# Two SBUF tiles for the exponentials of a two-map attention, and the keys' other 64 rows written by an SBUF-to-SBUF transfer

## The chip, the core and the metric

The kernel runs on one core of a Trainium2 chip. The metric is the device time of one execution in microseconds (us). TensorE (PE) does the matrix products, VectorE (DVE), ScalarE (ACT) and GpSimd (POOL) the elementwise work, and SyncE (SP) issues the transfers. Each engine runs its own instruction list in order and waits on semaphores. [...]

## The reference, cut to what matters

Two transformer blocks follow each other: `first_block` with two layers on 512 latent and 256 context tokens, and `second_block` with one layer. The change touches only the attention of `first_block`: 8 heads in each of the two layers, each head with two softmax maps of 64 dimensions whose difference weighs the values.

```python
def _diff_attn(qb, k_all, v_all, lam):
    s = jnp.einsum('bqhid,bkhid->bhiqk', qb.astype(jnp.float32) * ATTN_SCALE, k_all.astype(jnp.float32))
    p = jax.nn.softmax(s, axis=-1)
    a = p[:, :, 0] - lam * p[:, :, 1]
    return jnp.einsum('bhqk,bkhe->bqhe', a.astype(v_all.dtype), v_all)

def _diff_subln(o, g, lam_init):
    of = o.astype(jnp.float32)
    y = of * lax.rsqrt(jnp.mean(jnp.square(of), axis=-1, keepdims=True) + RMS_EPS) * g * (1.0 - lam_init)
    return y.reshape(o.shape[0], o.shape[1], D_ATTN).astype(o.dtype)
...
    y_attn = jax.nn.silu(ag) * _diff_subln(att, subln_g_l, lam_init)
```

Keys are the 256 context and the 512 latent ones, 768 together. In layer 0 the context tokens have queries too, which see the 256 context keys alone; layer 1 has latent queries only.

## The kernel before

A number is kept as the sum of a high and a low fp32r part, and a product is three matmuls. `unit` (L198) is one such projection: 48 matmuls of 128x512 for the latent tokens into a PSUM tile of tag `ps_m` and, where context is wanted, 48 of 128x256 into another. `ps_m` has four buffers; the score tile `ps_s`, the transposition tile `ps_t` and the output tile `ps_v` have one each.

`attention` (L465) goes over the heads. For each it makes four units (queries, keys, values, gate), evicts them (`evict_q`, `evict_k`, `evict_v`, and L487 for the gate `SG`), and calls `attend`. The order of instructions on every engine is set at compile time by a scheduler with its own timing estimates. It lays the four units of head h+1 among the score rounds of head h: PE works on them while DVE and ACT do a softmax. These matmuls (L166) are called the fill here. The weights of the fill are split into parts by ACT (`whi`, L159) and POOL (`wlo`, L139); a reduction for later gates (`gpr`, L802 on POOL and L803 on ACT) runs along.

A score round is one map of one tile of 128 queries: two or four score matmuls into `ps_s` (L394), the maximum on DVE (L399), its multiple (L401), the exponential on ACT (L408), the reciprocal of the sum (L410). Map 0's exponentials go to an SBUF tile `E0` with two buffers; map 1's are written in place into `ps_s`. L415 and L416 make the weighted difference, L416 reading `ps_s`, so that the score tile is free only after L416. The difference is transposed on PE (L423), split (L427, L428) and multiplied with V (L433). A head of layer 0 has eight rounds of 768 keys, called long, and then four of 256 keys, called context rounds; a head of layer 1 has eight long ones.

`evict_k` writes four tiles for a head, each with one buffer: KH0 and KH1 hold the high part of a map's 64 dimensions in both halves of the partitions, KL0 and KL1 the low part. ACT writes two halves (L350, L351), DVE casts the other two (L352, L353) and makes all four low halves (L139 under L355, L356). Since the tiles have one buffer, they are written after the last scores of the head before. The source `qr` and the tile `vT` of `evict_v` share one buffer too, so that L360, which reads the value unit out of `ps_m`, waits for the last of these DVE operations, and the fill that needs this `ps_m` buffer (the gate unit's, then the next head's) waits for L360.

At the end of a head, the sum of squares of 256 queries comes from two matmuls with ones (L446, L447); then follow L453 and a square root on ACT (L455), reciprocals on DVE (L460), a product into `SG` (L461) and a store (L463). `SG` has one buffer: the next head's gate (L251) waits for that store, and the `ps_m` buffer that L251 reads is awaited by a value unit of the fill. [rows 8] shows that chain.

Of the kernel before, what the change touches and what calls it, by code (L numbers as in the profile page):

```python
# [11 lines left out]
F32 = mybir.dt.float32  # L12
F32R = mybir.dt.float32r
BF16 = mybir.dt.bfloat16
AF = mybir.ActivationFunctionType
ALU = mybir.AluOpType
# [7 lines left out]
NT = NL + NCX  # L24
# [21 lines left out]
def mixer_stack_kernel(ctx: ExitStack, tc: tile.TileContext, a: dict, out: bass.AP):  # L46
    nc = tc.nc
# [14 lines left out]
    def ps_s():  # L62
        return pp.tile([128, 2, 512], F32, name="ps_s", tag="s", bufs=1)

    def ps_t():
        return pp.tile([128, 512], F32, name="ps_t", tag="t", bufs=1)

    def ps_v():
        return pp.tile([128, 512], F32, name="ps_v", tag="v", bufs=1)
# [68 lines left out]
    def sub_lo(lo, src, hi, eng):  # L138
        eng.tensor_tensor(lo, src, hi.bitcast(F32), op=ALU.subtract)  # L139
# [182 lines left out]
    def rope(tp, dst, ps):  # L322
        sh = tp.tile([128, NL], F32, name="rsh", tag="rsh", bufs=1)
        nc.vector.stream_shuffle(sh, ps, SWAP16)
        nc.vector.tensor_tensor(dst, ps, rope_c, op=ALU.mult)
        nc.gpsimd.tensor_tensor(sh, sh, rope_s, op=ALU.mult)
        nc.gpsimd.tensor_tensor(dst, dst, sh, op=ALU.add)
# [14 lines left out]
    def evict_k(ap_, aq, u):  # L342
        kr = aq.tile([128, NT], F32, name="qr", tag="qr", bufs=1)
        rope(aq, kr[:, NCX:], u.lat)
        nc.scalar.copy(kr[:, :NCX], u.cx)
        KH0 = ap_.tile([128, NT], F32R, name="KH0", tag="KH0", bufs=1)
        KH1 = ap_.tile([128, NT], F32R, name="KH1", tag="KH1", bufs=1)
        KL0 = ap_.tile([128, NT], F32R, name="KL0", tag="KL0", bufs=1)
        KL1 = ap_.tile([128, NT], F32R, name="KL1", tag="KL1", bufs=1)
        nc.scalar.copy(KH0[0:64], kr[0:64])  # L350
        nc.scalar.copy(KH1[64:128], kr[64:128])  # L351
        nc.vector.tensor_copy(KH0[64:128], kr[0:64])  # L352
        nc.vector.tensor_copy(KH1[0:64], kr[64:128])  # L353
        for half in (slice(0, 64), slice(64, 128)):
            sub_lo(KL0[half], kr[0:64], KH0[0:64], nc.vector)  # L355
            sub_lo(KL1[half], kr[64:128], KH1[64:128], nc.vector)  # L356
        return (KH0, KL0), (KH1, KL1)

    def evict_v(ap_, u, vT):
        nc.scalar.copy(vT[:, NCX:], u.lat)  # L360
# [15 lines left out]
    def attend(ap_, l, h, Q, K, V, SG, T):  # L376
        Q0, Q1 = Q
        Vh, Vl = V
        for qp in range(T // 256):
            nkt = 6 if qp < 2 else 2  # L380
            nk = nkt * 128
            ncol = nk // 2 if nkt == 6 else nk
            nch = nk // ncol
            aTh = ap_.tile([128, 6, 256], F32R, name="aTh", tag="aTh", bufs=1)
            aTl = ap_.tile([128, 6, 256], F32R, name="aTl", tag="aTl", bufs=1)
            for qi in range(2):
                q0 = qp * 256 + qi * 128
                es, ds = [], []
                for m, (Qm, Km) in enumerate(((Q0, K[0]), (Q1, K[1]))):
                    ps = ps_s()  # L390
                    for c in range(nch):
                        o = ps[:, c, :ncol]
                        for i, kp in enumerate(Km):
                            nc.tensor.matmul(  # L394
                                o, Qm[:, q0:q0 + 128], kp[:, c * ncol:(c + 1) * ncol], start=i == 0, stop=i == 1
                            )
                    sv = ps[:, :nch, :ncol]
                    mx = ap_.tile([128, 1], F32, name="mx", tag="mx", bufs=4)
                    nc.vector.reduce_max(mx, sv, axis=AX.XY)  # L399
                    nb = ap_.tile([128, 1], F32, name="nb", tag="nb", bufs=4)  # L400
                    nc.vector.tensor_scalar(nb, mx, -0.125, None, op0=ALU.mult)  # L401
                    if m == 0:
                        e = ap_.tile([128, NT], F32, name="E0", tag="E0", bufs=2)
                        e = e[:, :nk].rearrange("p (c n) -> p c n", c=nch)
                    else:
                        e = sv
                    d = ap_.tile([128, 1], F32, name="dn", tag="dn", bufs=4)
                    nc.scalar.activation(e, sv, AF.Exp, bias=nb, scale=0.125, accum_out=d)  # L408
                    r = ap_.tile([128, 1], F32, name="rd", tag="rd", bufs=4)
                    nc.vector.reciprocal(r, d)  # L410
                    es.append(e)
                    ds.append(r)
                nc.vector.tensor_tensor(ds[1], ds[1], neglam[l], op=ALU.mult)
                E0, E1 = es
                nc.vector.tensor_scalar(E0, E0, ds[0], None, op0=ALU.mult)  # L415
                nc.vector.scalar_tensor_tensor(E0, E1, ds[1], E0, op0=ALU.mult, op1=ALU.add)  # L416
                kt_of = lambda kt: E0[:, kt * 128 // ncol, kt * 128 % ncol:kt * 128 % ncol + 128]
                for r in range((nkt + 2) // 3):
                    n = min(3, nkt - 3 * r)
                    tp = ps_t()  # L420
                    for i in range(n):
                        kt = 3 * r + i
                        nc.tensor.transpose(tp[:, i * 128:(i + 1) * 128], kt_of(kt), ident)  # L423
                    tv = tp[:, :n * 128].rearrange("p (k d) -> p k d", k=n)
                    dh = aTh[:, 3 * r:3 * r + n, qi * 128:(qi + 1) * 128]
                    dl = aTl[:, 3 * r:3 * r + n, qi * 128:(qi + 1) * 128]
                    nc.scalar.copy(dh, tv)  # L427
                    nc.vector.tensor_tensor(dl, tv, dh.bitcast(F32), op=ALU.subtract)  # L428
            ov = ps_v()
            o = ov[:, :256]  # L430
            for kt in range(nkt):
                for p, (v, t) in enumerate(((Vh, aTh), (Vh, aTl), (Vl, aTh))):
                    nc.tensor.matmul(  # L433
                        o, v[:, kt], t[:, kt], start=(kt == 0 and p == 0), stop=(kt == nkt - 1 and p == 2)
                    )
            y = SG[:, qp * 256:(qp + 1) * 256]
            nc.vector.scalar_tensor_tensor(y, o, subg[l], y, op0=ALU.mult, op1=ALU.mult)
            o2 = ap_.tile([128, 256], F32, name="o2", tag="o2", bufs=1)
            nc.scalar.square(o2, o)
            o2h = ap_.tile([128, 256], F32R, name="o2h", tag="o2h", bufs=1)  # L440
            o2l = ap_.tile([128, 256], F32R, name="o2l", tag="o2l", bufs=1)
            nc.scalar.copy(o2h, o2)
            sub_lo(o2l, o2, o2h, nc.vector)
            msv = ps_v()
            ms = msv[:, :256]
            nc.tensor.matmul(ms, ones_r, o2h, start=True, stop=False)  # L446
            nc.tensor.matmul(ms, ones_r, o2l, start=False, stop=True)  # L447
            if qp == 0:
                rt = ap_.tile([128, 512], F32, name="rt", tag="rt", bufs=1)
                nc.scalar.copy(rt[:, :256], ms)  # L450
                continue
            r = slice(256, 512) if qp == 1 else slice(0, 256)
            nc.scalar.copy(rt[:, r], ms)  # L453
            n = 512 if qp == 1 else 256
            nc.scalar.activation(rt[:, :n], rt[:, :n], AF.Sqrt, bias=eps_t, scale=8.0)  # L455
            for i in range(n // 256):
                q0 = (0, 256)[i] if qp == 1 else 512
                ri = rt[:, i * 256:(i + 1) * 256]
                y = SG[:, q0:q0 + 256]
                nc.vector.reciprocal(ri, ri)  # L460
                nc.vector.tensor_tensor(y, y, ri, op=ALU.mult)  # L461
            o = 0 if qp == 1 else 512
            nc.sync.dma_start(Yd[4 + h][:, o:o + n], SG[:, o:o + n])  # L463
# [245 lines left out]
    with pool("start", R) as sp:  # L709
# [53 lines left out]
        for k in range(KT):  # L763
            hf = sp.tile([128, NT], F32, name="hf0", tag="hf0", bufs=2)
            for i, (nm, o, n, dst) in enumerate(halves):
                nc.vector.scalar_tensor_tensor(
                    hf[:, o:o + n], dst[k][:, 0].bitcast(F32), mods[nm][:, k:k + 1], dst[k][:, 1].bitcast(F32),
                    op0=ALU.add, op1=ALU.add,
# [524 lines left out]
```

## Time and profile before

| | |
|---|---|
| median of 3 runs | 3666.74 us (3661.18 to 3671.53) |
| profiled execution | 3662.99 us, span 3661.2 us |
| mean granted PE clock | 0.95 of 2.4 GHz |
| busy share | PE 90%, DVE 69%, POOL 56%, ACT 42% |
| attention, layer 0 | about 300 to 1150 us of the span |
| attention, layer 1 | about 1700 to 2350 us of the span |

A row of a timeline gives start, length, engine, line, operation, tile written <- tiles read, shapes, and in brackets the idle time before it with the instruction that ended it. Rows of waits give the waiting engine and tile, the releaser, then total us, times and longest.

### The profile page before, as it was taken

How to read it: one execution, taken by the hardware profiler on the slowest of the kernel's cores; microseconds unless marked ns; L12 is line 12 of the kernel's file. 1: busy time of each engine (PE TensorE's matmuls, PEld its weight loads, DVE VectorE, ACT ScalarE, POOL GpSimd, SP SyncE). 2: the span in 40 equal slices, each digit the busy share in tenths (PEclk: the TensorE clock that was granted, in tenths of full speed). 3: DMA queues.
4: the chain of work that ended last, by engine and by line, in shares of the span. 5: the costliest groups of instructions: out<-in, count | busy, mean ns of one | idle time of the engine just before them, and what ended most of it. 6: DMA issues, size and time to landing. Idle time of an engine off the chain costs nothing.

```text
span 3661.2 us, 47866 instructions
## 1 busy us (share of the span) xinstructions
PE 3285.1 (90%) x16462; PEld 2749.9 (75%) x16462; DVE 2541.2 (69%) x3849; ACT 1543.7 (42%) x3208; POOL 2054.8 (56%) x1420
## 2 busy tenths in 40 slices
PE   5879888889988879999999999999989899999987
PEld 4668677778877767777888888877768787878765
DVE  9994565565547888865555665477566889986676
ACT  4433655666433113233556554422445333335343
POOL 6665666777323453245777773478766544444432
PEclk8889899999999989999999999999999999999999
DMA  7542332233115556664444432287766222222575
GB/s 258 207 164 79 105 98 91 92 98 96 53 64 166 172 167 223 190 221 150 138 146 137 142 124 73 84 304 279 230 221 206 97 89 87 90 81 91 180 226 194
DMA packets 269140, 541.03 MB, mean 148 GB/s; under 512 B 30080, under 2 KB 37088, under 8 KB 260704
## 3 DMA queue, kind: packets, MB, share of 16 engines
q1 hardware_dynamic: 268896, 537.97, 45.0%
q8 instruction: 129, 2.11, 0.2%
q14 instruction: 115, 0.94, 0.1%
HBM read 508.05 MB, written 29.80 MB: 147 GB/s over the span
## 4 chain that ended last, share of the span: by engine, by line
PE 40%; DVE 26%; DMA 12%; issue 9%; POOL 9%; ACT 5%; SPq 1%; POOLq 0%; DVEq 0%; ACTq 0%
PE ps_m L166 30%; DVE acc L985 5%; DMA wraw<-in_w_out_dram 5%; POOL wlo L139 4%; DVE gpr L806 4%; POOL gpr L802 3%; DVE gjunk L292 2%; PE ps_s L394 2%; DVE wlo L139 2%; DMA gw<-in_w_ada_dram 2%; PE ps_v L433 1%; DVE h L139 1%; ACT whi L159 1%; PE ps_m L624 1%; PE ps_m L625 1%
## 5 line engine op out<-in xcount | busy, mean ns | idle before, releaser
L139 POOL TENSOR_TENSOR wlo<-wraw,whi 128x512 fp32r<-128x512 f32 x760 | 1120.2, 1491 | 936.5 <-ACT whi L159 819.8
L166 PE MATMUL ps_m<-h,whi 128*128 128x512 f32 (+1 forms) x4608 | 1571.3, 400 | 67.9 <-ACT vT L360 50.4
L166 PEld LDWEIGHTS ps_m<-h,whi 128*128 128x128 f32 x4608 | 880.4, 193 | 258.4 <-ACT vT L360 52.0
L159 ACT CAST whi<-wraw 128x512 fp32r<-128x512 f32 x1032 | 602.7, 618 | 790.9 <-DMA wraw<-in_w_out_dram 264.8
L166 PE MATMUL ps_m<-h,wlo 128*128 128x512 f32 (+1 forms) x2304 | 919.4, 400 | 0.1
L802 POOL TENSOR_TENSOR gpr<-gw,gv 128x512 f32<-128x512 f32 x320 | 429.6, 1342 | 242.5 <-ACT gpr L803 187.6
L166 PEld LDWEIGHTS ps_m<-h,wlo 128*128 128x128 f32 x2304 | 444.3, 193 | 93.6 <-POOL wlo L139 0.5
L166 PE MATMUL ps_m<-hc,whi 128*128 128x256 f32 x1920 | 510.4, 283 | 0.0
L139 DVE TENSOR_TENSOR wlo<-wraw,whi 128x512 fp32r<-128x512 f32 x272 | 240.4, 896 | 182.0 <-ACT whi L159 179.3
L166 PEld LDWEIGHTS ps_m<-hc,whi 128*128 128x128 f32 x1920 | 356.9, 191 | 4.0
L803 ACT ACTIVATE gpr<-gpr 128x512 f32<-128x512 f32 x320 | 201.6, 630 | 243.9 <-POOL gpr L802 243.1
L166 PE MATMUL ps_m<-hc,wlo 128*128 128x256 f32 x960 | 271.6, 283 | 0.0
L806 DVE SCALAR_TENSOR_TENSOR gpr<-gw,gv 128x512 f32<-128x512 f32 x264 | 263.4, 998 | 10.9 <-DMA gw<-in_w_mod_dram 2.5
L985 DVE SCALAR_TENSOR_TENSOR acc<-gu,pack,acc 128x511 f32<-128x511 f32 (+24 forms) x240 | 232.3, 980 | 5.4
L624 PE MATMUL ps_m<-wlo,y 128*128 128x512 f32 x512 | 207.2, 405 | 21.7 <-POOL wlo L139 13.7
L625 PE MATMUL ps_m<-whi,y 128*128 128x512 f32 x512 | 203.2, 398 | 1.5 <-DVE y L139 1.5
L399 DVE TENSOR_REDUCE mx<-ps_s 128x1 f32<-128x768 f32 (+1 forms) x160 | 135.0, 844 | 84.4 <-PE ps_s L394 83.5
L623 PE MATMUL ps_m<-whi,y 128*128 128x512 f32 x512 | 182.4, 399 | 2.5 <-ACT whi L159 2.3
L166 PEld LDWEIGHTS ps_m<-hc,wlo 128*128 128x128 f32 x960 | 183.4, 191 | 0.8
L240 PE MATMUL ps_m<-h,whi 128*128 128x512 f32 x320 | 126.6, 443 | 56.6 <-DVE h L139 29.1
L428 DVE TENSOR_TENSOR aTl<-ps_t,aTh 128x384 fp32r<-128x384 f32 (+1 forms) x144 | 77.5, 538 | 134.2 <-ACT aTh L427 133.6
L410 DVE RECIPROCAL rd<-dn 128x1 f32<-128x1 f32 x160 | 26.1, 163 | 191.9 <-ACT ps_s L408 99.0
(374 smaller groups left out, 5850.0 us busy)
## 6 DMA issues: line engine op xcount, KB each, us to landing
wraw<-in_w_in_dram SPq DMA_DIRECT2D x640, 256.0 KB, 2.9
wraw<-in_w_out_dram SPq DMA_DIRECT2D x384, 256.0 KB, 3.6
wm<-in_w_mod_dram SPq DMA_DIRECT2D x48, 1024.0 KB, 5.6
gw<-in_w_mod_dram SPq DMA_DIRECT2D x192, 256.0 KB, 3.5
gw<-in_w_ada_dram SPq DMA_DIRECT2D x136, 256.0 KB, 3.2
wm<-in_w_ada_dram SPq DMA_DIRECT2D x14, 1024.0 KB, 6.3
yraw<-yd SPq DMA_DIRECT2D x40, 256.0 KB, 3.4
gw<-in_w_gateT_dram SPq DMA_DIRECT2D x32, 256.0 KB, 3.1
```

The costliest lines, as they stand in the source:

```text
L139: eng.tensor_tensor(lo, src, hi.bitcast(F32), op=ALU.subtract)
L159: nc.scalar.copy(hi[:, sl], raw)
L166: nc.tensor.matmul(ps, w, mv[part], start=(first and p == 0), stop=(last and p == 2))
L240: nc.tensor.matmul(u.lat, wt, H[k][:, part], start=first, stop=last)
L399: nc.vector.reduce_max(mx, sv, axis=AX.XY)
L623: nc.tensor.matmul(ps, yh, hi[:, sl], start=(k == 0), stop=False)
L624: nc.tensor.matmul(ps, yh, lo[:, sl], start=False, stop=False)
L625: nc.tensor.matmul(ps, yl, hi[:, sl], start=False, stop=(k == KT - 1))
L802: nc.gpsimd.tensor_tensor(pr, w, t, op=ALU.mult)
L803: nc.scalar.activation(pr, pr, AF.Copy, scale=scale, accum_out=part[v][:, i:i + 1])
L806: nc.vector.scalar_tensor_tensor(junk, w, scale, t, op0=ALU.mult, op1=ALU.mult, accum_out=part[v][:, i:i + 1])
L985: nc.vector.scalar_tensor_tensor(A[:, s:], U[:, :NL - s], wj(i), A[:, s:], op0=ALU.mult, op1=ALU.add)
```

## The change

In `evict_k` a map's keys get one tile `K0` or `K1` of two planes, high and low, again with one buffer. ACT copies the 64 rows that the map's keys already stand in to the high plane, DVE makes the low plane of those rows, and one transfer, begun on GpSimd, copies both planes of these rows (64 x 1536 floats, 384 KB) to the other 64 rows. The two DVE casts and two of the four DVE subtractions of a head go; two transfers on POOL's list come, 32 in all. In `attend`, both maps' exponentials go to SBUF tiles `E0` and `E1` with one buffer each; the scaling is done on E1, and the difference is written over E0 from two SBUF operands. `ps_s` is free after the exponential.

```diff
-        KH0 = ap_.tile([128, NT], F32R, name="KH0", tag="KH0", bufs=1)
...
-        nc.scalar.copy(KH0[0:64], kr[0:64])
-        nc.scalar.copy(KH1[64:128], kr[64:128])
-        nc.vector.tensor_copy(KH0[64:128], kr[0:64])
-        nc.vector.tensor_copy(KH1[0:64], kr[64:128])
-        for half in (slice(0, 64), slice(64, 128)):
-            sub_lo(KL0[half], kr[0:64], KH0[0:64], nc.vector)
-            sub_lo(KL1[half], kr[64:128], KH1[64:128], nc.vector)
-        return (KH0, KL0), (KH1, KL1)
+        Ks = [ap_.tile([128, 2, NT], F32R, name=f"K{m}", tag=f"K{m}", bufs=1) for m in range(2)]
+        for m, Km in enumerate(Ks):
+            own, other = (slice(64 * i, 64 * i + 64) for i in (m, 1 - m))
+            nc.scalar.copy(Km[own, 0], kr[own])
+            sub_lo(Km[own, 1], kr[own], Km[own, 0], nc.vector)
+            nc.gpsimd.dma_start(Km[other], Km[own])
+        return [(Km[:, 0], Km[:, 1]) for Km in Ks]
...
-                    if m == 0:
-                        e = ap_.tile([128, NT], F32, name="E0", tag="E0", bufs=2)
-                        e = e[:, :nk].rearrange("p (c n) -> p c n", c=nch)
-                    else:
-                        e = sv
+                    e = ap_.tile([128, NT], F32, name=f"E{m}", tag=f"E{m}", bufs=1)
+                    e = e[:, :nk].rearrange("p (c n) -> p c n", c=nch)
...
-                nc.vector.tensor_scalar(E0, E0, ds[0], None, op0=ALU.mult)
-                nc.vector.scalar_tensor_tensor(E0, E1, ds[1], E0, op0=ALU.mult, op1=ALU.add)
+                nc.vector.tensor_scalar(E1, E1, ds[1], None, op0=ALU.mult)
+                nc.vector.scalar_tensor_tensor(E0, E0, ds[0], E1, op0=ALU.mult, op1=ALU.add)
```

The scheduler orders the changed program anew. The number of PE instructions stays, but the fill moves. In the changed kernel the scores are L389, the transpositions L415, the product with V L425, the ones matmuls L438 and L439, the transfer L351; the fill stays L166.

The first place is on PE in layer 1, between one head's last ones matmul and the value unit that waits for L251 of the next head (the last row of each fence; `h` tiles are the activations, `whi` and `wlo` the weights). Before, 81 rows lie between the two, most of them fill; the last nine are these:

```order
L166 MATMUL ps_m<-h_15_13893,whi 128x512
L166 MATMUL ps_m<-hc_15_14984,whi 128x256
L166 MATMUL ps_m<-h_15_13893,wlo 128x512
L166 MATMUL ps_m<-hc_15_14984,wlo 128x256
L394 MATMUL ps_s<-KH_16854,Q_16703 128x384 [waits DVE_49,PE_49]
L394 MATMUL ps_s<-KL_16856,Q_16703 128x384
L394 MATMUL ps_s<-KH_16854,Q_16703 128x384
L394 MATMUL ps_s<-KL_16856,Q_16703 128x384
L166 MATMUL ps_m<-h_0_13878,whi 128x512 [waits DVE_49]
```

After, from the ones matmuls on, this is all that lies between:

```order
L438 MATMUL ps_v<-o2h,ones_r 128x256 [waits Activation_49]
L439 MATMUL ps_v<-o2l,ones_r 128x256 [waits DVE_49]
L389 MATMUL ps_s<-K_17615,Q_17464 128x384 [waits Activation_49]
L389 MATMUL ps_s<-K_17615,Q_17464 128x384 x3
L415 MATMUL ps_t<-ident,E_17882 128x128 [waits DVE_49,PE_49]
L415 MATMUL ps_t<-ident,E_17882 128x128 x2
L415 MATMUL ps_t<-ident,E_17882 128x128 [waits DVE_49]
L415 MATMUL ps_t<-ident,E_17882 128x128 x2
L389 MATMUL ps_s<-K_17616,Q_17465 128x384 [waits Activation_49]
L389 MATMUL ps_s<-K_17616,Q_17465 128x384 x3
L166 MATMUL ps_m<-h_0_13894,whi 128x512 [waits DVE_49]
```

The fill that stood here has moved ahead of the ones matmuls. There are six such places, at six of the seven passages from head to head in layer 1. Before, 77 to 82 matmuls lie between, by the shapes 11.1 to 12.1 us of fill; after, 14 matmuls and no fill at each of the six.

The second place is on PE at the end of a head of layer 0, from the third context round to the fill that waits for L360 (its last row). Before, where the third round's score matmuls (`KH_4849`, ahead of the first row) are followed by 20 rows of fill, of which the last seven are shown:

```order
L166 MATMUL ps_m<-hc_14_161,wlo 128x256
L166 MATMUL ps_m<-h_15_146,whi 128x512
L166 MATMUL ps_m<-hc_15_162,whi 128x256
L166 MATMUL ps_m<-h_15_146,whi 128x512
L166 MATMUL ps_m<-hc_15_162,whi 128x256
L166 MATMUL ps_m<-h_15_146,wlo 128x512
L166 MATMUL ps_m<-hc_15_162,wlo 128x256
L446 MATMUL ps_v<-o2h,ones_r 128x256 [waits Activation_49]
L394 MATMUL ps_s<-KH_4850,Q_4695 128x256 [waits Activation_49]
L394 MATMUL ps_s<-KL_4852,Q_4695 128x256
L447 MATMUL ps_v<-o2l,ones_r 128x256 [waits DVE_49]
L166 MATMUL ps_m<-h_0_131,whi 128x512 [waits Activation_49]
```

After, the third and fourth context rounds, then the next head's first scores (`K_5818`), then the fill:

```order
L389 MATMUL ps_s<-K_4855,Q_4700 128x256 [waits Activation_49]
L389 MATMUL ps_s<-K_4855,Q_4700 128x256
L438 MATMUL ps_v<-o2h,ones_r 128x256 [waits Activation_49]
L415 MATMUL ps_t<-ident,E_5435 128x128 [waits DVE_49]
L415 MATMUL ps_t<-ident,E_5435 128x128
L439 MATMUL ps_v<-o2l,ones_r 128x256 [waits DVE_49]
L389 MATMUL ps_s<-K_4856,Q_4701 128x256 [waits PE_49,Activation_49]
L389 MATMUL ps_s<-K_4856,Q_4701 128x256
L389 MATMUL ps_s<-K_5818,Q_5663 128x384 [waits DMASW0_49,PE_49,Activation_49]
L389 MATMUL ps_s<-K_5818,Q_5663 128x384 [waits DVE_49]
L389 MATMUL ps_s<-K_5818,Q_5663 128x384 x2
L166 MATMUL ps_m<-h_0_131,whi 128x512 [waits Activation_49]
```

The fill has left the last three context rounds for the long rounds of the same head (by the shapes, some 13 us of it stand before, and 2.5 us after, between the first context scores and the awaited fill), and the first scores of the next head, which wait for the new transfer (`DMASW0`), stand ahead of the awaited fill instead of behind its beginning. So it is in heads 1 to 6 of layer 0; head 0 has a bare end in both kernels.

The third place is on POOL at that same end of a head, after the change; before, the two L351 rows are not there:

```order
L794 TENSOR_TENSOR gpr<-gw,gv_6588 128x512 [waits Activation_49]
L351 DMA K_5818<-K_5818 64x1536 [waits DMASW6_49,DVE_49]
L794 TENSOR_TENSOR gpr<-gw,gv_7710 128x512 [waits DMAHW1_49,DVE_49,Activation_49]
L794 TENSOR_TENSOR gpr<-gw,gv_7715 128x512 [waits DVE_49,Activation_49]
L351 DMA K_5819<-K_5819 64x1536 [waits DMASW7_49,DVE_49,PE_49]
L794 TENSOR_TENSOR gpr<-gw,gv_7710 128x512 [waits DMAHW2_49,Activation_49]
```

Each transfer waits on POOL for the DVE subtraction of its map (`DVE_49`), with `gpr` work queued behind it.

## Rows read from the trace of the kernel before

**Rows 1.** Page, busy time, share of the span and instructions of each engine.

```profile
PE 3285.1 (90%) x16462; PEld 2749.9 (75%) x16462; DVE 2541.2 (69%) x3849; ACT 1543.7 (42%) x3208; POOL 2054.8 (56%) x1420
```

**Rows 2.** Stretches of 50 us: busy time of the engines, granted clock, DMA share, GB/s.

```profile
550.00:600.00 50.00, 49.50 (x287) 44.02 (x288) 26.58 (x47) 29.04 (x71) 38.40 (x31) 0.97 0.31 95
600.00:650.00 50.00, 38.87 (x222) 33.95 (x220) 30.60 (x47) 30.57 (x73) 28.46 (x22) 0.90 0.29 90
2000.00:2050.00 50.00, 45.77 (x261) 40.00 (x260) 34.48 (x53) 31.24 (x73) 36.69 (x28) 0.97 0.41 130
```

**Rows 3.** PE's waits in attention of layer 0 (300 to 1150 us).

```profile
PE ps_m L166 <- ACT vT L360: 50.4, 7, 9.0
PE ps_m L166 <- ACT qr L333: 11.1, 4, 3.9
```

**Rows 4.** PE's waits from 1290 to 2370 us, the one that concerns the change.

```profile
PE ps_s L394 <- DVE E L416: 11.2, 5, 3.0
```

**Rows 5.** PE timeline, end of head 0 (first three rows) and of head 2, layer 0.

```profile
401.78 0.37 PE L394 MATMUL ps_s<-KH,Q 128*128 128x256 f32 x1
418.40 0.58 PE L394 MATMUL ps_s<-KH,Q 128*128 128x256 f32 x1 [4.99 <-ACT E L408]
425.79 1.22 PE L166 MATMUL ps_m<-h,whi 128*128 128x512 f32 x2 [6.59 <-ACT vT L360]
...
597.88 0.36 PE L394 MATMUL ps_s<-KH,Q 128*128 128x256 f32 x1
614.05 0.28 PE L394 MATMUL ps_s<-KH,Q 128*128 128x256 f32 x1
616.74 0.39 PE L447 MATMUL ps_v<-o2l,ones_r 128*128 128x256 f32 x1 [2.28 <-DVE o2l L139]
623.84 1.22 PE L166 MATMUL ps_m<-h,whi 128*128 128x512 f32 x2 [6.72 <-ACT vT L360]
```

**Rows 6.** PE timeline, the same fill shortly after that stall and later.

```profile
628.70 0.63 PE L166 MATMUL ps_m<-h,wlo 128*128 128x512 f32 x1
...
629.76 0.40 PE L166 MATMUL ps_m<-h,wlo 128*128 128x512 f32 x1
```

**Rows 7.** DVE timeline at the end of head 2, layer 0, beside [rows 5].

```profile
617.99 1.50 DVE L353 CAST KH<-qr 64x768 fp32r<-64x768 f32 x1
...
620.04 1.92 DVE L139 TENSOR_TENSOR KL<-qr,KH 64x768 fp32r<-64x768 f32 x2
```

**Rows 8.** Timelines, layer 1: the first passage (PE, DVE, SP), the last one's ends.

```profile
1853.93 0.39 PE L447 MATMUL ps_v<-o2l,ones_r 128*128 128x256 f32 x1 [0.34 <-DVE o2l L139]
...
1870.25 0.44 PE L394 MATMUL ps_s<-KH,Q 128*128 128x384 f32 x1 [2.19 <-DVE E L416]
...
1859.99 3.37 DVE L460 RECIPROCAL rt<-rt 128x256 f32<-128x256 f32 x2 [1.96 <-ACT rt L455]
...
1871.21 0.69 DVE L251 SCALAR_TENSOR_TENSOR SG<-rsh,ps_m 128x512 f32<-128x512 f32 x1 [1.01 <-DMA yd<-SG]
...
1867.41 0.38 SPq L463 DMA_DIRECT2D yd<-SG  x1
...
2227.28 0.37 PE L447 MATMUL ps_v<-o2l,ones_r 128*128 128x256 f32 x1
2237.64 0.69 DVE L251 SCALAR_TENSOR_TENSOR SG<-rsh,ps_m 128x512 f32<-128x512 f32 x1 [0.21 <-DMA yd<-SG]
```

**Rows 9.** Groups by line and shape, 300 to 2370 us: busy us, mean ns, idle before.

```profile
L139 DVE TENSOR_TENSOR KL<-qr,KH 64x768 fp32r<-64x768 f32 x64 | 80.7, 1261 | 4.6 <-ACT KH L351 2.5 <-ACT KH L350 1.2
L353 DVE CAST KH<-qr 64x768 fp32r<-64x768 f32 x16 | 16.7, 1045 | 10.7 <-PE ps_s L394 10.4
L416 DVE SCALAR_TENSOR_TENSOR E<-ps_s,rd,E 128x768 f32<-128x768 f32 x64 | 65.1, 1017 | 2.1
L629 DVE SCALAR_TENSOR_TENSOR r<-xr,r 128x512 f32<-128x512 f32 x24 | 20.8, 869 | 2.7 <-DMA xr<-in_x_dram 2.4
```

**Rows 10.** Page, transfers: KB each, median us from issue to landing.

```profile
yd<-SG SPq DMA_DIRECT2D x16, 256.0 KB, 2.1
...
rc<-in_rcount_dram SPq DMA_DIRECT2D x4, 384.0 KB, 5.5
```

More of the change, by code (lines that the diff above doesn't have):

```diff
@@ L345, in evict_k @@
         nc.scalar.copy(kr[:, :NCX], u.cx)
-        KH0 = ap_.tile([128, NT], F32R, name="KH0", tag="KH0", bufs=1)
-        KH1 = ap_.tile([128, NT], F32R, name="KH1", tag="KH1", bufs=1)
-        KL0 = ap_.tile([128, NT], F32R, name="KL0", tag="KL0", bufs=1)
-        KL1 = ap_.tile([128, NT], F32R, name="KL1", tag="KL1", bufs=1)
-        nc.scalar.copy(KH0[0:64], kr[0:64])
-        nc.scalar.copy(KH1[64:128], kr[64:128])
-        nc.vector.tensor_copy(KH0[64:128], kr[0:64])
-        nc.vector.tensor_copy(KH1[0:64], kr[64:128])
-        for half in (slice(0, 64), slice(64, 128)):
-            sub_lo(KL0[half], kr[0:64], KH0[0:64], nc.vector)
-            sub_lo(KL1[half], kr[64:128], KH1[64:128], nc.vector)
-        return (KH0, KL0), (KH1, KL1)
+        Ks = [ap_.tile([128, 2, NT], F32R, name=f"K{m}", tag=f"K{m}", bufs=1) for m in range(2)]
[5 more added lines that the diff above has]
+        return [(Km[:, 0], Km[:, 1]) for Km in Ks]
     def evict_v(ap_, u, vT):
```

## The prediction

> **What bounds the kernel now.** I read the busy shares first: PE is busy 90% of the span, DVE 69% [rows 1]. So an edit that only relieves DVE is worth what PE waits for DVE, and no more. The stretches of 50 us then show where PE waits: between two ends of heads it is full (49.50 of 50), and each end of a head in layer 0 costs some 11 us of idle PE and a lower mean granted clock, 0.90 [rows 2]. PE's waits name the cause: of layer 0's idle time 50.4 us in seven waits is the fill that waits for L360, and 11.1 us in four for L333 [rows 3]. In layer 1 the waits are small: 11.2 us in five for L416 [rows 4]. The ends of heads are therefore the only places where the change can act; in the long rounds fill covers the softmax in both kernels.
>
> **What the change removes and adds, off the path.** Per head two casts of 1.05 us (L353; L352 is its like) and two of four subtractions of 1.26 us go [rows 9]: 16 x (2.1 + 2.5) = 74 us of DVE. L416's successor reads two SBUF operands instead of PSUM and SBUF. The nearest row with two SBUF operands is L629, 869 ns for 512 columns, so 1.3 us for 768, against 1017 ns now [rows 9]: 64 x 0.3 = +19 us; at best it stays 1.02 us. DVE is some 55 us lighter of 2541. Where PE is full this gives nothing.
>
> `ps_s` is freed by the exponential rather than by L416: worth up to the 11.2 us of [rows 4], and I count that inside the places below, since these waits stand there. E0's single buffer makes the next tile's first exponential wait for the transpositions of this tile. In long rounds some 6 to 12 us of fill lies between, so I cost it at nothing; without that cover it would cost a round about a microsecond.
>
> The transfers: no row shows one begun by POOL. Bounds for 384 KB are the 2.1 us of a 256 KB store and the 5.5 us of a 384 KB load [rows 10]; I take 4. In layer 0 the next head's first scores wait for it ahead of the awaited fill. From the last map-0 scores the transfer needs a copy, a subtraction of 1.26, at most one POOL instruction, and its landing: some 4 + 4 = 8 us. The awaited fill comes some 12 us after those scores: 5 to the scores of map 1 (the stall of 4.99 ahead of them is of that kind) and 425.79 - 418.40 = 7.4 from there [rows 5]. So 4 us of cover remain and I cost it at nothing; one that lands in 10 us would cost 2 us a head. In layer 1 more than 20 us lie between.
>
> DVE is busy 27 to 31 of 50 us around the ends of heads [rows 2], and no row tells how a transfer that POOL begins fares beside it. The Trainium skill's page "SBUF — State Buffer", section "SBUF: two separate sides", speaks against one: its descriptors are written by GpSimd's cores, which are locked out of a port that they share with DVE while DVE runs a two-port operation. No run here shows this yet; by that rule the transfers would come late, and the time would be rival C's.
>
> **What it moves: layer 0.** The order takes fill out of the context rounds: 13 us of it stand there before, 2.5 after. The cover of the tail goes, and the tail itself gets shorter. Head 0 already shows a bare tail: from its first context scores to the awaited fill 401.78 to 425.79 = 24.0 us, of which 11.6 are two stalls (4.99 and 6.59 [rows 5]) and some 16 are stalls in all, with five small ones of 0.3 to 1.6. Head 2 with fill: 597.88 to 623.84 = 26.0 us, stalls 2.28 + 6.72 = 9.0 [rows 5]. So a bare tail is 2 us shorter and stalls 7 more. The change takes one cast (1.50) and two subtractions in the queue (1.92) out of the chain that ends in L360 [rows 7], and L416 out of the way to the next scores: up to 3.5 us. A bare tail is then 20.5 to 24 us; I take 22. PE's own work in it is 24.0 - 16 = 8, so it stalls 14 instead of 9: +5 a head. Half of the L333 waits go, since there is more fill in front: 11.1 / 2 over seven heads, -0.8. A longer stall leaves PE longer at the lower level of its clock, about +0.5. That is +4.7, for heads 1 to 6: **+28 us** (ends: 20.5 gives +19, 24 gives +40). Head 0 keeps its bare tail, 2 us shorter, but its fill now ends before the eighth long round, which costs about the 4 us that a round's chain takes: +2, together **+30**. If the small stalls shrink as well, the lower end is about zero.
>
> **What it moves: layer 1.** Here is the larger term. The chain from L447 to the end of L251 is 1871.90 - 1853.93 = 18.0 us in the first passage, with the reciprocals 6.1 us after L447, the store at 13.5, and L251 waiting for that store [rows 8]. The six passages give 18.0, 17.2, 18.4, 16.1, 16.0 and, last, 2238.33 - 2227.28 = 11.1 [rows 8]: 16.1 in the mean. 11 to 12 us of fill lie beside this chain, so that PE's longest stall in the first passage is 2.19 us [rows 8], and all stalls together are 2.5 us a passage in the mean of the six.
>
> After the change nothing of this fill is left between the ones matmuls and the value unit that waits for L251. PE has eight score matmuls and six transpositions, none longer than the 0.40 us of a 512-column matmul [rows 6]; their rows overlap, so 14 x 0.40 = 5.6 is the top, and I take 2.2. The chain itself stays: copy, square root, two reciprocals (3.37), two products, store, landing (2.1 [rows 10]; 3.8 from issue to L251 in the first passage), L251. A bare PE delivers its scores and transpositions sooner, so that DVE meets the links of the chain in a shorter queue; I take 13.5, between the 11.1 and the 16.1 above. The stall is 13.5 - 2.2 = 11.3, which is 8.8 more than now. Behind a long stall the fill runs at the lower clock level (1.2 of 2.4 GHz): one matmul takes 0.63 us until 5 us after it, then 0.40 [rows 6]; 5 us at half the pace lose some 2.5 us, of which today's shorter stalls lose perhaps 0.5. So +10.8 a passage, six of them: **+65 us**. Ends: 11.1 gives +6.4 and +1.5 for the clock, so +47; 16.1 gives +11.4 and +2.5, so +83.
>
> The fill that is moved ahead meets rounds in which PE has no idle time to fill (49.50 of 50 [rows 2]), so it earns nothing there.
>
> **Sum.** Profiled execution 3663.0 + 30 + 65 = 3758. The median of the runs is 3.75 us above the profiled one; with that (3666.74 - 3662.99), **3762 us**, +2.6%.
>
> **Rivals.** A, faster: the chains at the ends of heads collapse, because DVE's queue, not the order on PE, made them long. If without casts and L416 the bare tail of layer 0 falls to 15 us (stall 7 instead of 9), and layer 1's chain to 4 us, PE's own work covers it there. For it: L353 and KL stand directly ahead of L360 [rows 7]. Against it: two reciprocals of 3.37 us and the store stay in layer 1's chain, and alone with the landing make over 6. Layer 0 would give 7 x (-2) and -6 of the L333 waits, layer 1 its 15 us of stalls, and the clock some 10: 3667 - 45 = 3622 us. It decides from a layer 1 chain below 4.7 us.
>
> B, slower but little: layer 1's chain is like the last passage (11.0), and layer 0 comes out even, since the shorter tail pays for the lost cover: 3667 + 47 = 3714. It lies within my range.
>
> C, slower by more: the transfers are late. Each lands in 12 us rather than 4, since POOL, which is busy 38 of 50 us between the ends [rows 2], comes to it late or takes long to begin it, with `wlo` behind it; then the first scores of seven heads, and the fill that stands behind them on PE, come 4 us later, and in layer 1 the `wlo` parts: 14 x 4 = 56 on top, about 3818. For it: no row shows such a transfer; against it: the 2.1 to 5.5 of [rows 10]. It decides from 8 us of landing.
>
> D: the stalls are only renamed. PE's sum of work and idle time would stay and the time be within 0.3% (11 us, about what a measurement of this kernel can tell from no change): 3667. It needs layer 1's missing cover to be made up by idle time elsewhere, and PE idles there only 4.2 us of 50 even around a passage [rows 2].
>
> **How the numbers follow.** The forecast with its own ends (3667 + 47 + 0 = 3714 to 3667 + 83 + 42 = 3792) has 0.66, B 0.13, C 0.07, A 0.09, D 0.05. Leaving A, D and a part of C and B out, the range is 3695 to 3805. Faster by over 0.3% is A, 0.09; within 0.3% D with the lowest part of B, 0.07; slower 0.84.
>
> **What would show it.** In the changed profile, waits of PE at L166 for L251 of 8 to 13 us should stand six times in layer 1, with a granted clock near 0.85 in these stretches instead of 0.97. At the ends of heads in layer 0, the wait for L360 stays near 6 us, and waits of 3 to 5 us at the scores L389 for the exponential appear. No long wait should name a transfer of K; if one does, C holds. DVE's busy time falls by some 55 us. If layer 1's chain after the ones matmuls is under 8 us, or PE works on something else there, the main term is wrong. If bare tails in layer 0 are under 17 us, that term has the wrong sign.

## The result: 3.6% slower, and the profile after

The changed kernel takes 3798.23 us (3791.62 to 3800.03, four runs) against 3666.48 us: a ratio of 1.0356 (95% interval 1.0337 to 1.0376). The forecast was 3762 us, slower; the time lies in its range of 3695 to 3805, near the upper end, and the loss of 132 us is larger than the 95 that the sum gave.

The changed kernel's page: the line that answers to [rows 1], PE's busy share and granted clock in 40 slices of the span (in tenths), and the new transfer (KB each, median us from issue to landing):

```profile
PE 3328.7 (88%) x16462; PEld 2774.1 (73%) x16462; DVE 2476.9 (65%) x3785; ACT 1548.7 (41%) x3208; POOL 2091.2 (55%) x1452
...
PE   5779788889997879899988889989898899999997
...
PEclk8889889999998889999999889999999999999998
...
K<-K POOLq DMA_DIRECT2D x32, 384.0 KB, 5.1
```

DVE is 64 us lighter, as forecast (55), and the time rose all the same. PE has the same 16462 instructions; they take 43.6 us longer (3285.1 before), and its idle time, span less busy, is 466.6 us against 376.1. These two make up the 134.1 us by which the spans differ. Where the time went is seen when each kernel is cut at the first score matmuls of a layer's attention and at the last round of its eighth head. First the kernel before, then the changed one; columns as in [rows 2], first row layer 0, second layer 1:

```profile
336.27:1104.09 767.82, 684.32 (x3986) 603.63 (x3984) 428.32 (x751) 429.01 (x994) 458.13 (x347) 0.94 0.28 87
1762.26:2341.41 579.15, 561.15 (x3033) 481.90 (x3031) 343.48 (x544) 322.34 (x720) 385.09 (x288) 0.99 0.39 123
```

```profile
341.34:1156.91 815.57, 716.12 (x4049) 624.80 (x4048) 388.94 (x714) 431.20 (x994) 469.77 (x364) 0.92 0.30 90
1811.10:2494.78 683.68, 614.18 (x3180) 521.38 (x3180) 323.00 (x511) 331.70 (x728) 417.09 (x314) 0.94 0.40 117
```

Layer 1 is 105 us longer. Idle PE grew from 18.0 to 69.5 us there (length less PE's busy time), and PE's busy time by 53.0. Part of the latter is work that moved in: 151 more fill matmuls of 512 columns run in this stretch. PE's rows by shape, layer 1, the kernel before and then the changed one (count, busy us, mean ns, idle before):

```profile
L166 PE MATMUL ps_m<-h,whi 128*128 128x512 f32 x1049 | 361.0, 400 | 0.7 <-DVE SG L251 0.7
L166 PE MATMUL ps_m<-h,wlo 128*128 128x512 f32 x525 | 209.6, 399 | 0.0
```

```profile
L166 PE MATMUL ps_m<-h,whi 128*128 128x512 f32 x1150 | 393.4, 406 | 6.8 <-ACT vT L355 6.8
L166 PE MATMUL ps_m<-h,wlo 128*128 128x512 f32 x575 | 232.9, 405 | 0.0
```

At 0.23 us each (three in the 0.70 us from 2018.40 to 2019.10 below) they are some 35 us of work; some 18 of the 53 are left for the lower clock, whose mean fell from 0.99 to 0.94. Layer 0 is 48 us longer: 16 of idle time (83.5 to 99.5), some 13 of fill that moved in (46 more matmuls of 512 columns and 18 of 256), and some 19 left for the clock. The first scores start 5.1 us later, what lies between the two layers is 4 us shorter, and what lies behind is 19 us shorter: 105 + 48 + 5 - 4 - 19 = 135. These last are not gains, since they hold less work: of the 90.5 us of additional idle time 67.5 lie in the two stretches and 23 outside them, 13.6 of these behind layer 1's attention.

One passage of layer 1 in the changed kernel, PE from the last ones matmul on, then DVE and ACT (timelines):

```profile
1998.52 0.28 PE L439 MATMUL ps_v<-o2l,ones_r 128*128 128x256 f32 x1
1999.00 0.97 PE L389 MATMUL ps_s<-K,Q 128*128 128x384 f32 x4 [0.20 <-ACT E L400]
2003.41 0.78 PE L415 MATMUL ps_t<-ident,E 128*128 128x128 f32 x3 [3.43 <-DVE nb L396]
2007.77 0.90 PE L415 MATMUL ps_t<-ident,E 128*128 128x128 f32 x3 [3.58 <-DVE aTl L420]
2011.55 1.65 PE L389 MATMUL ps_s<-K,Q 128*128 128x384 f32 x4 [2.87 <-ACT E L400]
2012.99 1.05 PE L166 MATMUL ps_m<-h,whi 128*128 128x512 f32 x2
...
2018.40 0.63 PE L166 MATMUL ps_m<-h,whi 128*128 128x512 f32 x2
...
2019.10 0.63 PE L166 MATMUL ps_m<-h,whi 128*128 128x512 f32 x2
```

```profile
2000.03 1.90 DVE L408 SCALAR_TENSOR_TENSOR E<-E,rd,E 128x768 f32<-128x768 f32 x1
...
2003.18 0.14 DVE L396 TENSOR_SCALAR nb<-mx 128x1 f32<-128x1 f32 x1
2003.94 3.36 DVE L452 RECIPROCAL rt<-rt 128x256 f32<-128x256 f32 x2 [0.62 <-ACT rt L447]
...
2007.22 0.49 DVE L420 TENSOR_TENSOR aTl<-ps_t,aTh 128x384 fp32r<-128x384 f32 x1
...
2011.73 0.69 DVE L251 SCALAR_TENSOR_TENSOR SG<-rsh,ps_m 128x512 f32<-128x512 f32 x1
```

```profile
2009.21 1.28 ACT L400 ACT_TABLE_LOAD   x1
2010.50 0.90 ACT L400 ACTIVATE E<-ps_s,nb 128x768 f32<-128x768 f32 x1
```

PE idles 3.43 + 3.58 + 2.87 = 9.9 us between the ones matmul and the fill. The first wait follows a DVE queue of L408, the next round's maximum and the split of V (L366): the transpositions read what L408 writes, and they may write `ps_t` only when L366 has read it (the releaser named, L396, is the last of that queue). The second is for the split L420 behind the two reciprocals. The third is for an exponential behind the table load that leads back from the root. This exponential writes E0. Its maximum was ready at 2003.32 (the end of L396), but with one buffer it cannot start before the transpositions that read E0 have ended, at 2008.67. Then the fill starts without waiting: L251 ended 0.57 us before. From L439 to the end of L251 it is 2012.42 - 1998.52 = 13.9 us. The six passages without fill idle 8.5 to 10.6 us each, 59 of the stretch's 69.5. PE's longest waits of layer 1 (window 1811 to 2495 us):

```profile
PE ps_t L415 <- DVE aTl L420: 20.2, 6, 4.1
PE ps_s L389 <- ACT E L400: 19.5, 10, 2.9
PE ps_t L415 <- DVE nb L396: 10.3, 3, 3.4
PE ps_t L415 <- DVE Vl L366: 9.2, 3, 4.7
```

The end of head 2 of layer 0 in the changed kernel (PE timeline), which answers to the rows of head 2 in [rows 5]:

```profile
623.79 0.40 PE L389 MATMUL ps_s<-K,Q 128*128 128x256 f32 x2
...
632.21 0.50 PE L389 MATMUL ps_s<-K,Q 128*128 128x256 f32 x2 [0.70 <-ACT E L400]
...
635.61 0.80 PE L389 MATMUL ps_s<-K,Q 128*128 128x256 f32 x2 [0.61 <-ACT E L400]
642.72 1.65 PE L389 MATMUL ps_s<-K,Q 128*128 128x384 f32 x4 [6.32 <-ACT E L400]
```

From the first context scores it is 18.9 us to the next head's first scores and 21.0 to the awaited fill (644.79); the long wait is now for the exponential at those scores. It took the place of the wait for L360, which is L355 here, as PE's longest waits of layer 0 say. They answer to [rows 3] (window 336 to 1160 us):

```profile
PE ps_s L389 <- ACT E L400: 42.6, 17, 6.3
PE ps_m L166 <- ACT qr L333: 15.4, 6, 4.0
...
PE ps_m L166 <- ACT vT L355: 8.4, 4, 5.6
```

### The profile page after: what moved, and what is told of

The parts are those of the page before. It is cut to its first block, busy times and chain, and to the rows that moved or that the text cites. A ratio compares the mean times of both kernels' runs of the same rounds, so it can differ in the third digit from the quotient of the medians.

```text
span 3795.3 us, 47796 instructions
## 1 busy us (share of the span) xinstructions
PE 3328.7 (88%) x16462; PEld 2774.1 (73%) x16462; DVE 2476.9 (65%) x3785; ACT 1548.7 (41%) x3208; POOL 2091.2 (55%) x1452
## 4 chain that ended last, share of the span: by engine, by line
PE 39%; DVE 26%; DMA 11%; issue 9%; POOL 8%; ACT 6%; SPq 0%; DVEq 0%; POOLq 0%; ACTq 0%
PE ps_m L166 29%; DVE acc L977 5%; DMA wraw<-in_w_out_dram 4%; DVE gpr L798 4%; POOL gpr L794 3%; POOL wlo L139 3%; DVE gjunk L292 2%; DVE wlo L139 2%; DMA gw<-in_w_ada_dram 2%; PE ps_s L389 2%; ACT whi L159 2%; DVE h L139 1%; PE ps_v L425 1%; PE ps_m L616 1%; ACT gpr L795 1%
## 5 line engine op out<-in xcount | busy, mean ns | idle before, releaser
L139 POOL TENSOR_TENSOR wlo<-wraw,whi 128x512 fp32r<-128x512 f32 x760 | 1133.5, 1509 | 954.5 <-ACT whi L159 823.0
L166 PE MATMUL ps_m<-h,whi 128*128 128x512 f32 (+1 forms) x4608 | 1573.4, 402 | 43.1 <-ACT qr L333 15.4
L166 PEld LDWEIGHTS ps_m<-h,whi 128*128 128x128 f32 x4608 | 885.2, 195 | 235.9 <-ACT vT L355 18.8
L166 PE MATMUL ps_m<-h,wlo 128*128 128x512 f32 (+1 forms) x2304 | 923.1, 401 | 0.7 <-POOL wlo L139 0.7
L166 PEld LDWEIGHTS ps_m<-h,wlo 128*128 128x128 f32 x2304 | 446.3, 194 | 95.9 <-POOL wlo L139 1.1
L166 PE MATMUL ps_m<-hc,whi 128*128 128x256 f32 x1920 | 508.1, 285 | 0.0
L166 PEld LDWEIGHTS ps_m<-hc,whi 128*128 128x128 f32 x1920 | 356.3, 192 | 3.8
L166 PE MATMUL ps_m<-hc,wlo 128*128 128x256 f32 x960 | 272.4, 284 | 0.0
L420 DVE TENSOR_TENSOR aTl<-ps_t,aTh 128x384 fp32r<-128x384 f32 (+1 forms) x144 | 77.6, 539 | 296.5 <-ACT aTh L419 296.5
L798 DVE SCALAR_TENSOR_TENSOR gpr<-gw,gv 128x512 f32<-128x512 f32 x264 | 254.3, 963 | 13.0 <-DMA gw<-in_w_mod_dram 5.3
L616 PE MATMUL ps_m<-wlo,y 128*128 128x512 f32 x512 | 206.2, 403 | 21.8 <-POOL wlo L139 12.1
L389 PE MATMUL ps_s<-K,Q 128*128 128x384 f32 x576 | 139.9, 363 | 68.4 <-ACT E L400 62.1
L166 PEld LDWEIGHTS ps_m<-hc,wlo 128*128 128x128 f32 x960 | 183.6, 191 | 0.7
```

The costliest lines, as they stand in the source:

```text
L166: nc.tensor.matmul(ps, w, mv[part], start=(first and p == 0), stop=(last and p == 2))
L389: nc.tensor.matmul(o, Qm[:, q0:q0 + 128], kp[:, c * ncol:(c + 1) * ncol], start=i == 0, stop=i == 1)
L616: nc.tensor.matmul(ps, yh, lo[:, sl], start=False, stop=False)
L798: nc.vector.scalar_tensor_tensor(junk, w, scale, t, op0=ALU.mult, op1=ALU.mult, accum_out=part[v][:, i:i + 1])
```

## The experiments

Two theories stood: **O**, that E0's single buffer made the scheduler pull the fill ahead, so that PE meets the ends of heads bare; and its rivals, **K**, the transfers, and **S**, the difference from two SBUF operands with E1 in SBUF. (PSUM, where map 1's exponentials stood before, is what PE writes its products to; in these traces DVE and ACT read it.) All ratios are to the kernel before, run beside it.

**The exponentials alone.** The changed kernel with `evict_k` as before.

> The change of the exponentials alone (both maps in SBUF, one buffer each), the keys as before. Theory O (E0's single buffer moves the fill out of the ends of heads, and the bare chains stall PE): the order has 14 matmuls and no fill in five of the six passages of layer 1, as the changed kernel has, so nearly the whole loss stands here: 3785 us (3770 to 3805), PE idle in layer 1 about 70 us against 18 before. Rival K (the transfers of the keys cost the time): 3670 to 3690, since no transfer is left.

3823.41 us, ratio 1.0449 (1.0427 to 1.0470). Without any transfer the loss is larger than with them: K is not needed for it. The size was missed by 38 us.

**The keys alone.** The kernel before with the new `evict_k`.

> The change of the keys alone (transfers begun on GpSimd), the exponentials as before. Theory O: the fill stays in the passages (78 to 87 matmuls of it by the order), so no loss: 3660 us (3640 to 3675), perhaps a gain from the DVE operations that no longer stand ahead of L360. Rival K: 3740 or more.

3611.61 us, ratio 0.9872 (0.9854 to 0.9890): a clear gain, more than expected. PE's longest wait of layer 0, to be read beside [rows 3]:

```profile
PE ps_m L166 <- ACT vT L355: 28.0, 6, 6.5
```

The wait for the copy of the value unit, 50.4 us before, is 28.0. Four of a head's six DVE operations on the keys no longer stand in front of it; that this is the reason is not shown, and the last experiment speaks against it.

**One buffer alone.** The kernel before with one number changed.

```diff
-                        e = ap_.tile([128, NT], F32, name="E0", tag="E0", bufs=2)
+                        e = ap_.tile([128, NT], F32, name="E0", tag="E0", bufs=1)
```

> The kernel before with one edit: E0 has one buffer instead of two; map 1's exponentials stay in PSUM, keys as before. Theory O: the order loses the fill in the passages of layer 1 (14 to 30 matmuls left of 77 to 82) and in two context rounds, so 3775 us (3745 to 3800). Rival S (reading both operands of the weighted difference from SBUF, or freeing the score tile early, costs the time): 3665 to 3680, since neither is in this kernel.

3773.55 us, ratio 1.0316 (1.0299 to 1.0333), as O expected. Its two stretches of attention (columns as in [rows 2]):

```profile
336.40:1143.90 807.50, 697.32 (x4046) 612.95 (x4045) 405.85 (x751) 431.76 (x1000) 454.73 (x349) 0.92 0.26 83
1784.10:2470.00 685.90, 615.32 (x3191) 522.06 (x3190) 336.89 (x544) 333.20 (x735) 401.33 (x301) 0.94 0.34 109
```

Layer 1 is the changed kernel's within about 2 us: 70.6 us idle, clock 0.94. So one buffer fewer is enough for the whole of layer 1's loss, with map 1's exponentials still in PSUM. It is not all that the exponentials' edit did: that edit as a whole, beside the same kernel before, is 50 us slower than this one (3823.41). With one buffer for E0, then, the rest of that edit (E1 in SBUF, the difference from two SBUF operands) costs too; how is not shown.

**Keys by VectorE in the changed kernel.** The transfer's line replaced by two copies.

```diff
-            nc.gpsimd.dma_start(Km[other], Km[own])
+            for i in range(2):
+                nc.vector.tensor_copy(Km[other, i], Km[own, i].bitcast(F32))
```

> The changed kernel with the 32 transfers replaced by 64 copies on VectorE. Theory O: the order keeps its bare passages, so the time stays near the changed kernel's 3798: 3800 us (3785 to 3820), the extra 2 copies a map costing a few us at the ends of heads in layer 0. Rival K: 3700 or less, as no transfer is left to wait for.

3787.12 us, ratio 1.0350 (1.0331 to 1.0368): as the changed kernel's 1.0356. K falls.

**Two buffers again.** E0's second buffer needs 3 KB a partition that the attention does not have free. It was first taken from the raw weights and the squares.

```diff
-                    e = ap_.tile([128, NT], F32, name=f"E{m}", tag=f"E{m}", bufs=1)
+                    e = ap_.tile([128, NT], F32, name=f"E{m}", tag=f"E{m}", bufs=2 - m)
...
-        raw = wp.tile([128, 512], F32, name="wraw", tag="wraw", bufs=4)
+        raw = wp.tile([128, 512], F32, name="wraw", tag="wraw", bufs=3)
```

> The changed kernel with E0 in two buffers again, E1 in SBUF with one. The 3 KB a partition come from three buffers instead of four for the raw weights and from the squares (o2) being written into the free half of rt. Theory O (one buffer of E0 moves the fill): by the order 10 to 28 us of fill stand in every passage of layer 1 again and 12 us in the tails of layer 0, so the loss goes whole: 3600 us (3580 to 3640). Rival S (E1 in SBUF and the difference from two SBUF operands cost the rest): 3690 or more.

> Control for the run before: the changed kernel with the same room made (three raw weight buffers, squares in rt) but E0 still with one buffer. All theories: as the changed kernel, 3798 us (3780 to 3815). If it is much faster, the room-making itself works and the other run tells less.

3633.07 us (ratio 0.9925, 0.9903 to 0.9947) with two buffers, 3857.54 us (1.0535, 1.0518 to 1.0552) for the control with one. The second buffer is worth 224 us between these two. The control missed its number by 60 us: three raw buffers cost something outside the attention. From the end of layer 1's attention on, control and changed kernel:

```profile
2500.10:3855.00 1354.90, 1209.95 (x5351) 955.82 (x5349) 935.42 (x1329) 485.16 (x946) 689.65 (x473) 0.96 0.47 160
```

```profile
2494.80:3795.00 1300.20, 1181.17 (x5351) 953.43 (x5349) 966.42 (x1329) 480.35 (x946) 705.88 (x473) 0.96 0.51 167
```

54.7 us of the difference lie there, so the room was then taken from the squares alone.

```diff
-            o2 = ap_.tile([128, 256], F32, name="o2", tag="o2", bufs=1)
+            if qp == 0:
+                rt = ap_.tile([128, 512], F32, name="rt", tag="rt", bufs=1)
+            o2, o2h, o2l = rt[:, 256:], aTh[:, 0], aTl[:, 0]
...
```

> Both edits of the change, E0 in two buffers, and all four raw weight buffers kept: the 3 KB come from the sums of squares alone (o2 in the free half of rt, its high and low part in the first 256 columns of aTh and aTl, which are done with by then). Theory O: the loss of the change was E0's single buffer and nothing else of the two edits, so this is as the run with three raw buffers less what those cost behind the attention (1390 us there against 1327 in the run of the keys alone): 3572 us (3550 to 3600), faster than before and than the keys alone. Rival S (E1 in SBUF or the two SBUF operands cost by themselves): not below the 3612 of the keys alone.

> The same with the keys as before, so the edit of the exponentials with E0 in two buffers alone. Theory O: an earlier free score tile is a gain where E0 has its two buffers: 3615 us (3590 to 3640). The difference to the run with both edits is then the gain of the keys' edit, about 45 us as it was alone. Rival S: 3665 or more.

> Control for both: the changed kernel with the room made in the same way, E0 still with one buffer. All theories: as the changed kernel, 3798 us (3780 to 3815), since the order keeps its bare passages.

| keys | E1 | E0 buffers | us | ratio (95% interval) |
|---|---|---|---|---|
| new | SBUF | 2 | 3579.67 | 0.9782 (0.9768 to 0.9797) |
| before | SBUF | 2 | 3599.56 | 0.9842 (0.9825 to 0.9858) |
| new | SBUF | 1 (control) | 3789.04 | 1.0362 (1.0342 to 1.0381) |

All three came as O expected. S falls as a cause by itself: with two buffers, both maps' exponentials in SBUF are a gain of 1.6%; a cost of E1 in SBUF showed only beside an E0 with one buffer. The second buffer is worth 209 us with both edits, and 113 in the kernel before. The two stretches of attention of the first of these kernels:

```profile
341.00:1019.10 678.10, 644.85 (x3863) 571.43 (x3861) 434.04 (x711) 418.21 (x982) 468.93 (x358) 0.99 0.35 104
1684.50:2248.10 563.60, 546.25 (x2958) 466.94 (x2958) 328.01 (x508) 314.49 (x706) 384.89 (x296) 0.99 0.45 134
```

Idle PE in layer 0 is 33 us, in the kernel before 83.5, and the clock is 0.99. The wait for L360, 50.4 us before, is not among PE's longer waits there any more.

**The square root left out.** In the changed kernel and in the kernel before, a copy in place of L447 and L455.

```diff
-            nc.scalar.activation(rt[:, :n], rt[:, :n], AF.Sqrt, bias=eps_t, scale=8.0)
+            nc.scalar.copy(rt[:, :n], rt[:, :n])
```

> The changed kernel with the square root of the normalisation left out (a copy stands in its place), so that its two table loads of 1.28 us a head (one into the root, one back to the exponential) go; the order keeps its bare passages. Theory O (bare chains through ACT and DVE set the ends of heads): about 2 to 3 us less at six passages and seven tails and some clock: 3755 us (3735 to 3775). Rival (the stall hangs on transfers or on the engine PE itself): 3790 or more.

> Control: the kernel before with the same square root left out. Theory O: 11 us of fill lie beside the chain in layer 1, so little is won there (at most the 2.5 us of stalls a passage), and in layer 0 the L360 wait may lose part of it: 3645 us (3630 to 3660), clearly less than the gain in the changed kernel. Rival: the same gain in both kernels.

3770.07 us (ratio 1.0287, 1.0261 to 1.0313) and 3630.52 us (0.9917, 0.9899 to 0.9935): 28 us off the changed kernel, 32 off the kernel before. The second half of the expectation, a clearly smaller gain in the kernel before, is wrong; this pair does not tell the theories apart. The trace of the first still tells how the two chains of a passage stand to each other (PE timeline, changed kernel without the root):

```profile
2060.74 0.87 PE L415 MATMUL ps_t<-ident,E 128*128 128x128 f32 x3 [3.44 <-DVE nb L396]
2064.39 0.90 PE L415 MATMUL ps_t<-ident,E 128*128 128x128 f32 x3 [2.78 <-DVE aTl L420]
2067.00 1.65 PE L389 MATMUL ps_s<-K,Q 128*128 128x384 f32 x4 [1.70 <-ACT E L400]
2069.65 0.80 PE L166 MATMUL ps_m<-h,whi 128*128 128x512 f32 x1 [1.00 <-DVE SG L251]
```

The wait for the exponential falls from 2.87 to 1.70, about the one table load, and now the fill waits 1.00 for L251. In the changed kernel the chain of the softmax round and the chain to L251 end within a microsecond of each other, so cutting one gives little.

**The best kernel with the keys by VectorE.** Both edits with two buffers, transfers replaced by copies.

> Both edits with E0 in two buffers, but the 32 transfers of the keys replaced by 64 copies on VectorE, so that the keys' gain is told apart: is it the transfer or only the new order of work? If the gain of the keys' edit is work taken off VectorE ahead of L360, this is slower than with the transfers: 3595 us (3580 to 3610). If the transfers' own latency costs (5 us ahead of head 0 of layer 0 in the changed kernel) and VectorE has room, it is faster: 3570 us.

3563.84 us, ratio 0.9749 (0.9729 to 0.9770), the fastest of all: the other side of the expectation. So the gain of the keys' edit does not need the transfer. DVE has as many operations as in the kernel before (3849), so their number is not the reason either; what is stays open. PE's busy time is the same in the two kernels (3259.5 and 3259.3 us), and the 19 us by which their spans differ are idle time: 7 before 300 us, 9 in layer 0's attention and 7 behind layer 1's, less 3 between the layers. One PE row of the kernel with transfers waits for one, at the end of head 0:

```profile
419.63 1.62 PE L389 MATMUL ps_s<-K,Q 128*128 128x384 f32 x4 [3.51 <-DMA K<-K]
```

## Why the prediction was right, and where its sizes were off

**The mechanism.** Right: the order loses the fill at the ends of heads, and PE waits there (59 of layer 1's 69.5 us of idle time). That E0's single buffer is what moved the order, the prediction did not say; it put that buffer at nothing, "since in long rounds 6 to 12 us of fill lies between". That step failed: with that one number changed the kernel before loses 3.2%. The price of the buffer was paid in the places that the fill had left; there the exponential that waits for E0 costs PE up to 2.87 us a passage, where the prediction had "about a microsecond" for a round without cover. What the runs do not separate is how much of the loss is the order and how much the wait itself: each kernel with one buffer had both.

That the sum came out near owes something to luck. In the attention it gave 95 us, and some 105 were measured (idle time and clock, without the work that moved), with layer 0's two terms off in opposite directions. The other 29 or so lie outside the two stretches, 23 of them idle time, and the prediction had nothing there.

**Layer 1, idle.** The forecast was six stalls of 11.3 us after a chain of 13.5. The six chains are 13.9, 13.9, 14.6, 14.6, 12.0 and 11.7 us, 13.5 in the mean, and the stalls in each sum to 8.5 to 10.6, since PE's own matmuls take more than the 2.2 us of the sum (0.97 + 0.78 + 0.90 + 1.65 = 4.3 in the passage shown); over the stretch idle PE grew by 51.5, against 6 x 8.8 = 53. The name of the wait was wrong: no wait for L251 of 8 to 13 us stands at L166. PE waits a few microseconds each at L415, L415 and L389, since the softmax rounds without fill are as long as the chain; only without the root does L251 come last.

**Layer 1, clock.** Mis-sized, though not by much: 2 us a passage, 12 in all, were forecast; some 18 were found above. In the stretch from 2000 to 2050 us, with one passage, the granted clock is 0.86, as forecast for it, against 0.97 in [rows 2]. First that stretch, then parts of the time around the passage:

```profile
2000.00:2050.00 50.00, 40.14 (x204) 34.16 (x205) 30.37 (x45) 29.08 (x65) 37.56 (x28) 0.86 0.42 127
```

```profile
1995.00:2003.40 8.40, 4.77 (x28) 3.89 (x27) 7.00 (x11) 6.64 (x16) 5.45 (x5) 1.00 0.33 94
2003.40:2007.00 3.60, 0.78 (x3) 0.38 (x3) 3.06 (x2) 1.71 (x4) 2.77 (x3) 0.52 0.51 176
...
2019.00:2023.00 4.00, 4.00 (x31) 3.82 (x30) 3.91 (x5) 1.00 (x2) 1.93 (x2) 1.00 0.10 35
```

The sum used 5 us of fill at half the pace behind one long stall [rows 6], and the fill does run so from 2012.99 to about 2017.5 (two matmuls in 1.05 us, 0.63 later). What it left out are the matmuls between the stalls: the clock is at its lower level (1.2 GHz) from the end of the first stall on, and the four scores at 2011.55 take 1.65 us, against 0.97 at 1999.00.

**Layer 0.** The tail was to take 20.5 to 24 us, 22 as the middle, with 14 of stalls. In heads 1 to 6 it takes 18.5 to 25.1, 21.1 in the mean; in head 2 it is 21.0, and 10.3 of them are stalls, against 9.0 before. So its length was right and the idle time of the forecast too large. The wait for L360 did not stay near 6 us, as was forecast: it went from 50.4 to 8.4 in all. The waits for the exponential took its place with 42.6 us in 17, and the longest of them, 6.3 in head 2, stands behind the root and two table loads on ACT. Measured are +16 us of idle time, where about 27 were forecast, and some 19 of clock, where 3 were; that clock term, 0.5 us a head, is the most mis-sized of the sum.

**The transfers.** Rightly put at no cost: none of PE's waits in the changed kernel's two stretches names one. They land in 5.1 us in the median (3.5 to 7.4), within the 2.1 to 5.5 taken from [rows 10]. POOL at the beginning of layer 0's attention:

```profile
337.12 0.73 POOL L351 DMA_DIRECT2D K<-K  x1 [2.16 <-DVE K L139]
```

The first scores start at 341.34 instead of 336.27, 4.2 us after that transfer was begun, but PE is not idle from 300 us to its first scores in either kernel: in the changed one fill stands ahead of them, 236 PE instructions instead of 198.

**DVE.** The difference from two SBUF operands takes 1482 ns in the mean in the changed kernel, 1017 before [rows 9]; 1.3 us were forecast. The loss does not need it, as the kernel with one buffer alone shows. The Trainium skill's page "SBUF — State Buffer", section "SBUF: two separate sides", says that a DVE operation with two SBUF inputs and a GpSimd operation that reads SBUF exclude each other on a shared port. The 1.90 us of L408 at 2000.03 above agree, POOL being at work on `gpr` until 2001.12 and on `wlo` from 2001.07; L408 at 2018.51, begun while POOL was idle, took 1.00. The Trainium skill's rule in the same section on transfers begun on GpSimd, that a two-port operation of DVE can hold up their descriptors, does not explain the longest landing here: the transfer begun at 1808.29 landed after 7.4 us, and DVE had no work in the 1.5 us after it was begun.

**Rivals.** A needed chains under 4.7 us in layer 1, and the shortest is 11.7. B needed 11.1 in the mean there and found 13.5. C's 3818 us are nearer to the measured time than the forecast's 3762, but C fell with the kernels without transfers: a time near a rival's does not make the rival true. D falls with the idle time and the clock.

## What to carry to other kernels

In a kernel whose order a scheduler makes, count a lost buffer by the order that comes out, not by the wait at the buffer: here one of two 3 KB buffers cost 3% where no single new wait is over 7 us. Test two edits that come together apart, and with the buffer given back: here one gained 1.3%, the other lost 4.5% with one buffer and gained 1.6% with two, and both with two buffers gain 2.2%. Compare stretches of two orders by idle time, not by length alone, since work moves between them. Look for room in tiles that are done with at that point, before taking a buffer that another stage needs.

## What had not been expected of the hardware

- PE stands at its lower clock level already after the first stall of a passage, of 3.43 us: the granted clock is 1.00 up to 2003.40, 0.52 from there to 2007.00, and 1.00 again from 2019 on, after work without a gap since 2011.55. Three stalls of 2.9 to 3.6 us give a stretch of 50 us 0.86, where one of 6.7 us gives 0.90 [rows 2].
- A transfer begun on GpSimd within SBUF (384 KB, 64 rows to 64 rows) occupies POOL for 0.57 us in the median and lands 3.5 to 7.4 us after its beginning.
- Three raw weight buffers instead of four cost 55 us behind the attention in the control, and 5 us up to there.
